# The opening of a two-layer diffusion block: the last 512 tokens loaded later, the modulation in four column groups, new orders on the engines

## The chip, the core and the metric

The kernel runs on one core of a Trainium2 chip. The metric is the device time of one execution in microseconds (us); three runs before the change gave 2850.42, 2852.49 and 2852.70, so the median is 2852.49. Engines: PE (TensorE, matrix products), DVE (VectorE), ACT (ScalarE), POOL (GpSimd) and SP (SyncE, which issues the transfers). PEld in the profile is PE's weight load.

## The reference

Two layers run on 1280 tokens of 1024 features, 256 of them context tokens and 1024 latent tokens. What bears on the change is the head of a layer:

```python
mod = silu_c @ w_ada[l] + b_ada[l]
sh1, sc1, g1, sh2, sc2, g2 = jnp.split(mod[:, None, :], N_MOD, axis=-1)
h = rmsnorm(x, norm1_g[l]) * (1.0 + sc1) + sh1
y, yc = token_mixers(h @ w_in[l], hc @ w_in[l], ...)
x = x + g1 * (y @ w_out[l])
```

The context goes through the same weights, with a modulation vector of its own. The mixers are a two-directional mLSTM, whose keys, values and gates are columns of `w_in`, and a neighbourhood attention. After them come the output projection, a squared-ReLU MLP of 4096 features with the other half of the modulation, and at the end a last RMSNorm. Everything is computed in fp32.

## The kernel before

Activations lie with features on the partitions: x is held in tiles of 128 features. Tokens come in three groups: group 0 is the 256 context tokens, group 1 the next 512, group 2 the last 512. In units of 128 tokens there are ten token tiles, in five pairs i = 0 to 4; pair 0 is group 0, pairs 1 and 2 are group 1, pairs 3 and 4 group 2. An fp32 product of activations and weights is made of three products of rounded parts (L94, L95, L96): the high part of each factor (`ah`, `whi`: a rounding copy on ACT) and the rest (`al`, `wlo`: a subtraction on DVE), without low times low.

The opening (function `opening`) is the stretch up to the first products of the mixers. It runs in layer 0 alone, in a part where each compute engine executes in the order in which the code is written. Its work:

- x is loaded in six transfers (L1566): x_146 and x_147 are group 0 (512 KB each), x_148 and x_149 group 1 and x_150 and x_151 group 2 (1024 KB each); the first of each pair holds features 0 to 511, which the code calls A, the other features 512 to 1023, B.
- Weights of keys, values and gates (`w_kvg`) come in three chunks (L1624, L1688), of 432, 432 and 288 KB, and are split into `whi` (L88) and `wlo` (L89).
- The modulation (`ada`) has two generators. `first` makes the shift and scale of A, `second` those of B. Each has eight k-steps: a load of 512 KB (`wada`, L169) into a ring of six buffers, and products with silu (L158) of 32 columns of PE. Here one k-step is two column groups with 512 columns each. I call the k-steps f0 to f7 and s0 to s7. Then come a copy of the sum (`arow`, L180), four transposes (L183), the addition of the bias (L187) and the gain (L220).
- `squares` (L1639 on ACT, L1640 on DVE, L1641 on PE with a matrix of ones) and `rstd` (L279, L280 on ACT) give the factor of each token; `scale` (L1646, DVE) multiplies it on, eight tiles per group.
- `norm` applies the modulation, in turns on ACT (L1658) and DVE (L1656), and makes the high part (L1094, ACT) and the low part (L1095, DVE).
- `project_g` multiplies pairs of token tiles by 288 columns, 12 products per tile and half of the features. Pairs 0, 1 and 2 are projected in the opening, in PSUM banks tagged "q"; pairs 3 and 4 in the mixers, in banks tagged "mm".

The mixers begin with two small transfers of silu to DRAM (`sscr`, L1572: 1024 elements each, 4 KB, written one 4-byte element at a time from 128 partitions), further modulation work (`fill`, four blocks of 256 columns per load, products in "q" banks), the tables of cosines and sines, and the keys: DVE applies the rotation (L450 to L454), PE transposes (L507), ACT copies.

On SP the built order is not quite the order of the code: a load that waits for a buffer is placed later, and issues written after it can stand ahead of it. Once placed, SP issues one after the other.

Of the kernel before, what the change touches and what calls it, by code (L numbers as in the profile page):

```python
# [11 lines left out]
F32 = mybir.dt.float32  # L12
# [14 lines left out]
KT = D // 128  # L27
# [14 lines left out]
def xf(x, gi, f, o=0, n=None):  # L42

    n = n or GROUPS[gi][1]
    return x[gi][f][:, o:o + n] if len(x[gi]) == KT else x[gi][f // 4][:, f % 4, o:o + n]


class Kern:
# [93 lines left out]
    def ada(self, l, blocks, tag, pool=None, bufs=1):  # L142

        nc, d, ws = self.nc, self.d, []
        pool, nb = pool or self.cp, len(blocks)
        if 0 in blocks:
            self.mod, self.A = self.cp.tile([128, 48, 2], F32, name="mod", bufs=2), {}
        mod = self.mod
        acc = self.bank(tag)
        n = 1024 // nb  # L150
        todo = [(k, o) for o in range(0, 512, n) for k in range(KT)]

        two = 2 if bufs == 1 else 1

        def through(k, o, w):
            for z in range(two):
                for j in range(nb):
                    nc.tensor.matmul(acc[32 * j:32 * j + 32, o:o + n], self.silu[:, k + z, :], w[:, z, j, :], start=k + z == 0, stop=k + z == KT - 1,  # L158
                                     skip_group_check=True, tile_position=(0, 32 * j))

        for i in range(0, len(todo) + bufs * two, two):
            if i >= bufs * two:
                through(*todo[i - bufs * two], ws.pop(0))
            if i < len(todo):
                k, o = todo[i]
                w = pool.tile([128, two, nb, n], F32, name="wada", bufs=bufs)
                for z in range(two):
                    src = d["w_ada"][l, (k + z) * 128:(k + z + 1) * 128, :].rearrange("p (b c) -> p b c", c=512)
                    nc.sync.dma_start(w[:, z], src[:, blocks[0]:blocks[-1] + 1:blocks[1] - blocks[0], o:o + n])  # L169
                    if z < two - 1:  # L170
                        yield
                ws.append(w)
            yield
        m = 32 * len(blocks)
        if bufs == 1:
            row = pool.tile([128, two, nb, n], F32, name="wada")
            rv = row[:].rearrange("p z b c -> p (z b c)")
        else:
            rv = pool.tile([128, 512], F32, name="arow")
        nc.vector.tensor_copy(rv[:m, :512], acc[:m, :])  # L180
        tp = self.bank(tag)
        for t in range(4):
            nc.tensor.transpose(tp[:, t * m:(t + 1) * m], rv[:m, t * 128:(t + 1) * 128], self.ident[:m, :m])  # L183
        for j, b in enumerate(blocks):
            src = tp[:, :4 * m].rearrange("p (t c) -> p t c", t=4)[:, :, 32 * j:32 * j + 2]
            fs = slice(4 * b, 4 * b + 4)
            nc.vector.tensor_add(mod[:, fs, :], src, self.bada[l][:, fs].unsqueeze(2).to_broadcast([128, 4, 2]))  # L187
            for v in range(2):
                self.gain(l, b, v)
        yield  # L190
# [270 lines left out]
    def mlstm_kv(self, l, hi, lo, W, accs):  # L461

        self.kv_begin(0)
        for i in range(NT // 2):
            ga = accs[i] if i in accs else self.project_g(W, i, hi, lo)
            for u in range(2):
                self.nc.scalar.copy(self.gr[:, 2 * i + u, :, 0:8], ga[u][:, 256:288].rearrange("p (q h) -> p q h", q=4))
            self.kv_take(0, i, ga)
            if i > 1:
                self.kv_turn(0, i - 2)  # L470
            yield
        self.kv_turn(0, NT // 2 - 2)
        self.kv_turn(0, NT // 2 - 1)
        yield
        for i in range(NT // 2):
            self.kv_weigh(0, i)
            self.kv_state(0, i)
            yield
        self.kv_back(0)
        yield  # L480
# [1131 lines left out]
    def opening(self, xp, ap0, xsrc, hi, lo):  # L1612


        nc, d = self.nc, self.d
        self.wide, self.ntmp = 0, 8
        x = self.alloc_x(xp, (0, 1, 2))
        self.setup()
        self.load_x(x, xsrc, (0, 1, 2))
        chunks, raws = ((0, 864), (864, 864), (1728, 576)), []  # L1620
        for o, n in chunks:
            raws.append(self.wp.tile([128, 1024], F32, name="wraw", bufs=WRAW) if o < 1728 else ap0.tile([128, n], F32, name="wraw2"))
        for z in range(2):
            nc.sync.dma_start(raws[z][:, :864], d["w_kvg"][0][:, z * 864:z * 864 + 864])  # L1624
        first, second = (self.ada(0, blocks, "mm", ap0, 6) for blocks in ((0, 2), (1, 3)))

        def steps(g, n):
            for _ in range(n):
                next(g)

        steps(first, 6)

        def squares(gi, q):
            p, n = self.bank("mm"), GROUPS[gi][1]
            q.extend((p, n))
            for f in range(0, KT, 2):
                sq = [self.sp.tile([128, 512], F32, name="tmp", bufs=self.ntmp) for _ in range(2)]
                for z, t in enumerate(sq):
                    nc.scalar.activation(t[:, :n], xf(x, gi, f + z), AF.Square)  # L1639
                nc.vector.tensor_add(sq[0][:, :n], sq[0][:, :n], sq[1][:, :n])  # L1640
                nc.tensor.matmul(p[:, :n], self.ones[:], sq[0][:, :n], start=f == 0, stop=f == KT - 2)  # L1641
                yield

        def scale(gi, r, fs=range(KT)):
            for f in fs:
                nc.vector.tensor_mul(xf(x, gi, f), xf(x, gi, f), r[:, :GROUPS[gi][1]])  # L1646

        def norm(todo):

            sh = self.mod[:, 0:8, :]  # L1650

            def modulation(gi, f):
                xs, v = xf(x, gi, f), 1 if gi == 0 else 0
                a, b = self.A[0][:, f, v:v + 1], sh[:, f, v:v + 1]
                if f % 2:
                    nc.vector.tensor_scalar(xs, xs, a, b, ALU.mult, ALU.add)  # L1656
                else:
                    nc.scalar.activation(xs, xs, AF.Identity, bias=b, scale=a)  # L1658

            modulation(*todo[0])  # L1660
            for n, (gi, f) in enumerate(todo):
                if n + 1 < len(todo):
                    modulation(*todo[n + 1])
                self.normed = self.parts(xf(x, gi, f), hi[f][gi][:], lo[f][gi][:])

        q, A, B, accs = [[], [], []], range(4), range(4, 8), {}
        run_all(squares(0, q[0]))
        run_all(squares(1, q[1]))
        r0 = self.rstd(*q[0])
        rest = squares(2, q[2])  # L1670
        steps(rest, 2)
        r1 = self.rstd(*q[1])
        scale(0, r0)
        steps(first, 1)
        steps(rest, 1)
        steps(first, 1)
        steps(rest, 1)
        for z in range(2):
            self.less_last(raws[z], chunks[z][1], 288)
        r2 = self.rstd(*q[2])  # L1680
        scale(1, r1)
        W = [self.split_raw(raws[z], chunks[z][1]) for z in range(2)]
        scale(2, r2, range(6))
        for z in range(6):
            steps(first, 1)
            steps(second, 1)
            if z == 3:
                nc.sync.dma_start(raws[2][:], d["w_kvg"][0][:, 1728:])  # L1688
        steps(first, 1)
        norm([(gi, f) for gi in range(2) for f in A])  # L1690
        scale(2, r2, range(6, 8))
        self.less_last(raws[2], chunks[2][1], 288)
        W.append(self.split_raw(raws[2], chunks[2][1]))
        steps(second, 3)
        accs[0] = self.project_g(W, 0, hi, lo, "q", ks=A, us=(0,))
        steps(second, 1)
        self.project_g(W, 0, hi, lo, "q", accs[0], A, (1,))

        steps(second, 4)
        accs[1] = self.project_g(W, 1, hi, lo, "q", ks=A, us=(0,))  # L1700
        steps(second, 1)
        self.project_g(W, 1, hi, lo, "q", accs[1], A, (1,))
        accs[2] = self.project_g(W, 2, hi, lo, "q", ks=A)
        norm([(gi, f) for gi in range(2) for f in B])
        norm([(2, f) for f in (*A, *B)])
        for i in range(3):
            self.project_g(W, i, hi, lo, "q", accs[i], B)
        return W, accs, self.value_weights(0, range(1))

    def run(self):  # L1710
# [147 lines left out]
def run_all(g):  # L1858
    for _ in g:
        pass  # L1860
# [148 lines left out]
```

## Time and profile before

| what | us |
|---|---|
| median of three runs | 2852.49 |
| the profiled execution's own time | 2852.3 |
| its span from first to last instruction | 2850.2 |
| PE busy in it | 2808.8 (99%) |
| DVE busy | 2199.9 (77%) |
| ACT busy | 1276.3 (45%) |
| first modulated x (L1658) | 38.25 |
| first projection (L94) | 40.30 |
| first modulated x of B (L1656) | 51.56 |

The mean granted clock of PE is 0.997. The rows of the timeline give start, duration, engine, line, operation, tiles, shapes, and in brackets the idle time of the engine just before with what ended it. A row with "x4" joins four like instructions, whose duration is then the sum or the stretch they cover.

### The profile page before, as it was taken

The numbers are of one execution on the slowest core, as the hardware profiler recorded it, in microseconds if no ns is written. First come the engines' busy times: TensorE is split into PE (matmuls) and PEld (weight loads), VectorE is DVE, ScalarE is ACT, GpSimd is POOL, SyncE is SP. The second block draws the span as 40 slices with busy tenths as digits, with TensorE's granted clock in tenths as the row PEclk, the third lists the DMA queues.
The fourth block names the chain that finished last, engine by engine and source line by source line (L and its number), as shares of the span: only waits on it lengthen the run. The fifth ranks groups of instructions, "written<-read, shape, count | busy, mean of one in ns | idle before, by whom it ended". The sixth has DMA issues, their size and how long they took to land. (4 is left out here: it accounts for less than half of the span.)

```text
span 2850.2 us, 45474 instructions
## 1 busy us (share of the span) xinstructions
PE 2808.8 (99%) x16500; PEld 2371.3 (83%) x16500; DVE 2199.9 (77%) x4909; ACT 1276.3 (45%) x2472; POOL 111.5 (4%) x191
## 2 busy tenths in 40 slices
PE   8999999999999999999999999999999999999998
PEld 4877778888888888888889988878888788888888
DVE  6779988776698777689878778878776887768774
ACT  5333335564553333444545333336564533344453
POOL 0110000011000000000000101000020000000000
PEclk9999999999999999999999999999999999999999
DMA  8433433336347555798977222223345454479672
GB/s 259 144 117 120 143 100 101 92 120 212 133 150 245 197 188 201 244 351 292 325 259 272 72 79 88 71 71 119 118 151 197 131 183 158 142 263 319 205 253 96
DMA packets 279264, 497.40 MB, mean 175 GB/s; under 512 B 23648, under 2 KB 119904, under 8 KB 279040
## 3 DMA queue, kind: packets, MB, share of 16 engines
q1 hardware_dynamic: 279040, 494.50, 51.9%
q8 instruction: 130, 2.13, 0.3%
q14 instruction: 94, 0.77, 0.1%
HBM read 398.82 MB, written 95.59 MB: 173 GB/s over the span
## 5 line engine op out<-in xcount | busy, mean ns | idle before, releaser
L94 PE MATMUL q<-ah,whi 128*128 128x512 f32 (+1 forms) x1472 | 549.4, 373 | 0.3 <-ACT whi L1094 0.3
L96 PE MATMUL q<-ah,wlo 128*128 128x512 f32 (+1 forms) x1472 | 547.0, 372 | 0.7 <-DVE wlo L1095 0.5
L95 PE MATMUL q<-al,whi 128*128 128x512 f32 (+1 forms) x1472 | 547.6, 372 | 0.0
L94 PE MATMUL mm<-ah,whi 128*128 128x512 f32 (+1 forms) x1120 | 387.1, 346 | 0.4 <-DVE nq L841 0.2
L95 PE MATMUL mm<-al,whi 128*128 128x512 f32 (+1 forms) x1120 | 384.8, 344 | 0.0
L96 PE MATMUL mm<-ah,wlo 128*128 128x512 f32 (+1 forms) x1120 | 384.6, 343 | 0.0
L94 PE MATMUL mm<-whi,ah 128*128 128x512 f32 (+2 forms) x864 | 317.9, 368 | 1.5 <-ACT va L792 1.5
L96 PEld LDWEIGHTS q<-ah,wlo 128*128 128x128 f32 x1472 | 277.2, 188 | 50.0 <-DVE wlo L1095 1.3
L94 PEld LDWEIGHTS q<-ah,whi 128*128 128x128 f32 x1472 | 277.4, 188 | 49.6 <-issue 1.7
L95 PEld LDWEIGHTS q<-al,whi 128*128 128x128 f32 x1472 | 277.5, 189 | 48.3 <-issue 1.4
L95 PE MATMUL mm<-wlo,ah 128*128 128x512 f32 (+2 forms) x864 | 307.4, 356 | 1.8 <-DVE wlo L89 1.7
L96 PE MATMUL mm<-whi,al 128*128 128x512 f32 (+2 forms) x864 | 307.2, 356 | 0.0
L94 PEld LDWEIGHTS mm<-ah,whi 128*128 128x128 f32 x1120 | 212.0, 189 | 28.2 <-issue 2.0
L96 PEld LDWEIGHTS mm<-ah,wlo 128*128 128x128 f32 x1120 | 212.0, 189 | 25.1 <-issue 0.2
L95 PEld LDWEIGHTS mm<-al,whi 128*128 128x128 f32 x1120 | 212.0, 189 | 24.7 <-issue 0.2
L1094 ACT CAST ah<-raw 128x512 fp32r<-128x512 f32 (+1 forms) x264 | 143.4, 566 | 124.1 <-PE q L96 51.5
L94 PEld LDWEIGHTS mm<-whi,ah 128*128 128x128 f32 x864 | 163.0, 189 | 27.5 <-ACT va L792 2.1
L96 PEld LDWEIGHTS mm<-whi,al 128*128 128x128 f32 x864 | 163.0, 189 | 23.8
L95 PEld LDWEIGHTS mm<-wlo,ah 128*128 128x128 f32 x864 | 163.3, 189 | 22.7 <-DVE wlo L89 3.1
L1095 DVE TENSOR_TENSOR al<-raw,ah 128x512 fp32r<-128x512 f32 (+1 forms) x264 | 157.4, 620 | 30.1 <-ACT ah L1094 29.9
L94 PE MATMUL q<-th,whi 128*128 128x512 f32 x384 | 150.3, 392 | 2.1 <-DVE s L1259 2.0
L95 PE MATMUL q<-x,whi 128*128 128x512 f32 x384 | 150.6, 392 | 1.1 <-DVE x L1095 1.1
(306 smaller groups left out, 5177.3 us busy)
## 6 DMA issues: line engine op xcount, KB each, us to landing
raw<-w SPq DMA_DIRECT2D x168, 512.0 KB
raw<-hid SPq DMA_DIRECT2D x104, 512.0 KB
wada<-w_adaT SPq DMA_DIRECT2D x96, 512.0 KB
wraw<-w SPq DMA_DIRECT2D x80, 512.0 KB
hid<-hb SPq DMA_DIRECT2D x128, 256.0 KB
hid<-ht SPq DMA_DIRECT2D x96, 256.0 KB
w<-gscr SPq DMA_DIRECT2D x36, 512.0 KB
wada<-w_ada SPq DMA_DIRECT2D x32, 512.0 KB
```

The lines of the kernel that those rows point to most:

```text
L94: mm(out, lh, rh, start=start, stop=False, skip_group_check=True)
L95: mm(out, lh, rl, start=False, stop=False, skip_group_check=True)
L96: mm(out, ll, rh, start=False, stop=stop, skip_group_check=True)
L1094: ins = self.nc.scalar.copy(hi, src)
L1095: self.nc.vector.tensor_sub(lo, src, fview(hi))
```

## The change

1. x_150 and x_151 (group 2) and the third chunk of `w_kvg` are loaded after eight loads of the modulation's first half.
2. A generator with two blocks now uses four column groups with 256 columns each, where it used two with 512. The copy is 128x256, and two transposes of 128x128 take the place of four.
3. The orders of all engines are written anew. The squares of group 2 stand on ACT behind the norms of groups 0 and 1 for A; on PE its four sums of squares are interleaved with projections for A and with s0 to s2. The third chunk's low part and three of the scales of group 2 follow, then the end of `second`. For B, norm and projection go group by group; the other five scales of group 2 stand after the norm of group 1, ahead of the norm of group 2.
4. Pair 3 is projected in the opening, with the two token tiles in turns. Pair 4 uses "q" banks, in both layers.

```diff
@@ ada: through
+            if nb == 2:
+                for g in range(4):
+                    nc.tensor.matmul(acc[32 * g:32 * g + 32, 0:256], self.silu[:, k, :], w[:, 0, g // 2, g % 2 * 256:g % 2 * 256 + 256], start=k == 0, stop=k == KT - 1,
+                                     skip_group_check=True, tile_position=(0, 32 * g))
+                return
@@ ada: end
-            rv = pool.tile([128, 512], F32, name="arow")
+            rv = pool.tile([128, 256], F32, name="arow")
+            nc.vector.tensor_copy(rv[:], acc[:, 0:256])
+            tp = self.bank(tag)
+            for t in range(2):
+                nc.tensor.transpose(tp[:, t * 128:(t + 1) * 128], rv[:, t * 128:(t + 1) * 128], self.ident)
...
@@ mlstm_kv
-            ga = accs[i] if i in accs else self.project_g(W, i, hi, lo)
+            ga = accs[i] if i in accs else self.project_g(W, i, hi, lo, "q" if i else "mm")
@@ opening
-        self.load_x(x, xsrc, (0, 1, 2))
+        self.load_x(x, xsrc, (0, 1))
...
+        def project(i, ks, u):
+            accs[i] = self.project_g(W, i, hi, lo, "q", accs.get(i), ks, (u,))
...
+        steps(first, 1)
+        self.load_x(x, xsrc, (2,))
+        nc.sync.dma_start(raws[2][:], d["w_kvg"][0][:, 1728:])
...
+        norm([(0, f) for f in A])
+        for u in range(2):
+            project(0, A, u)
+        rest = squares(2, q[2])
+        norm([(1, f) for f in A])
+        for i in (1, 2):
+            for u in range(2):
+                steps(rest, 1)
+                project(i, A, u)
+                steps(second, 1)
+        r2 = self.rstd(*q[2])
         W.append(self.split_raw(raws[2], chunks[2][1]))
-        steps(second, 3)
...
+        steps(second, 4)
+        scale(2, r2, range(3))
         steps(second, 1)
...
+        norm([(0, f) for f in B])
+        for u in range(2):
+            project(0, B, u)
+        norm([(1, f) for f in B])
+        for i in (1, 2):
+            for u in range(2):
+                project(i, B, u)
+        scale(2, r2, range(3, KT))
+        norm([(2, f) for f in range(KT)])
+        accs[3] = [self.bank("mm") for _ in range(2)]
+        for k in range(KT):
+            for u in range(2):
+                project(3, (k,), u)
         return W, accs, self.value_weights(0, range(1))
```

Line numbers in the order of the changed kernel are its own: L1584 is the load of x, L174 that of w_ada, L1590 the small transfer, L1657 the square, L1676 and L1674 the modulation on ACT and DVE, L1112 and L1113 the high and low parts, L1664 the scale, L185 the copy.

SP's issues from the loads of group 2 on, before:

```order
L1566 DMA x_150<-xT 128x4x512
L1566 DMA x_151<-xT 128x4x512
L1624 DMA wraw<-w_kvg 128x864 x2
L169 DMA wada<-w_ada 128x2x512 x12
L1688 DMA wraw_176<-w_kvg 128x576
L169 DMA wada<-w_ada 128x2x512 x4
L74 DMA wraw<-w_nv 128x1024
L1572 DMA sscr<-silu 128x8x1 x2
L169 DMA wada<-w_ada 128x4x256 x2
```

and with the change, from the first weights on:

```order
L1642 DMA wraw<-w_kvg 128x864 x2
L174 DMA wada<-w_ada 128x2x512 x8
L1584 DMA x_150<-xT 128x4x512
L1584 DMA x_151<-xT 128x4x512
L1698 DMA wraw_174<-w_kvg 128x576
L174 DMA wada<-w_ada 128x2x512 x6
L1590 DMA sscr<-silu 128x8x1 x2
L174 DMA wada<-w_ada 128x4x256
L174 DMA wada<-w_ada 128x2x512 x2
L74 DMA wraw<-w_nv 128x1024 x2
```

The 2 MB of group 2 have moved behind f7. The last two loads of the modulation, s6 and s7, which stood ahead of the two small transfers, now stand behind them and behind one load of the fill.

ACT, from the norm of group 1 for A to the norm of group 0 for B, with the change:

```order
L1112 CAST ah_91<-x_148 128x512
L1112 CAST ah_94<-x_148 128x512
L1112 CAST ah_97<-x_148 128x512
L1657 ACTIVATE tmp<-x_150 128x512 x4
L1657 ACTIVATE tmp<-x_151 128x512 x4
L297 ACTIVATE ssq<-mm,eps 128x512
L298 ACTIVATE ssq<-ssq 128x512
L88 CAST whi<-wraw_174 128x576
L1676 ACTIVATE x_147<-x_147,mod,A_333 128x256
```

The eight squares of group 2 and its factor stand here; before, they stood ahead of all norms, directly behind the squares of group 1.

DVE, from the last low parts of group 1 for B to the first of group 2, with the change:

```order
L1113 TENSOR_TENSOR al_130<-x_149,ah_106 128x512
L1113 TENSOR_TENSOR al_133<-x_149,ah_109 128x512
L1664 TENSOR_TENSOR x_150<-x_150,ssq 128x512
L1664 TENSOR_TENSOR x_151<-x_151,ssq 128x512 x4
L1674 TENSOR_SCALAR x_150<-x_150,A_333,mod 128x512
L1113 TENSOR_TENSOR al_113<-x_150,ah_89 128x512
```

Of the five scales in the middle, three stood ahead of the first half's copy in before, and two ahead of the third chunk's low part, so all of them ahead of the norms of B.

More of the change, by code (lines that the diff above doesn't have):

```diff
@@ L178, in ada @@
         else:
-            rv = pool.tile([128, 512], F32, name="arow")
+            rv = pool.tile([128, 256], F32, name="arow")
[3 more added lines that the diff above has]
+                nc.tensor.transpose(tp[:, t * 128:(t + 1) * 128], rv[:, t * 128:(t + 1) * 128], self.ident)
+            for j, b in enumerate(blocks):
+                fs = slice(4 * b, 4 * b + 4)
+                src = tp[:, 0:256].rearrange("p (t j h c) -> p j h t c", t=2, j=2, h=2)[:, j, :, :, 0:2]
+                nc.vector.tensor_add(mod[:, fs, :].rearrange("p (h t) v -> p h t v", h=2), src,
+                                     self.bada[l][:, fs].rearrange("p (h t) -> p h t", h=2).unsqueeze(3).to_broadcast([128, 2, 2, 2]))
+                for v in range(2):
+                    self.gain(l, b, v)
+            yield
+            return
         nc.vector.tensor_copy(rv[:m, :512], acc[:m, :])
@@ L1666, in opening @@
         q, A, B, accs = [[], [], []], range(4), range(4, 8), {}
+        def project(i, ks, u):
+            accs[i] = self.project_g(W, i, hi, lo, "q", accs.get(i), ks, (u,))
         run_all(squares(0, q[0]))
-        run_all(squares(1, q[1]))
+        more = squares(1, q[1])
+        steps(more, 2)
         r0 = self.rstd(*q[0])
-        rest = squares(2, q[2])
-        steps(rest, 2)
+        steps(more, 1)
+        steps(first, 1)
+        steps(more, 1)
+        steps(first, 1)
+        self.load_x(x, xsrc, (2,))
+        nc.sync.dma_start(raws[2][:], d["w_kvg"][0][:, 1728:])
         r1 = self.rstd(*q[1])
         scale(0, r0)
[L1674 to L1677, printed above, removed]
         for z in range(2):
             self.less_last(raws[z], chunks[z][1], 288)
-        r2 = self.rstd(*q[2])
-        scale(1, r1)
+        scale(1, r1, A)
         W = [self.split_raw(raws[z], chunks[z][1]) for z in range(2)]
-        scale(2, r2, range(6))
+        scale(1, r1, B)
         for z in range(6):
@@ L1686, in opening @@
             steps(second, 1)
-            if z == 3:
-                nc.sync.dma_start(raws[2][:], d["w_kvg"][0][:, 1728:])
+        self.less_last(raws[2], chunks[2][1], 288)
         steps(first, 1)
-        norm([(gi, f) for gi in range(2) for f in A])
-        scale(2, r2, range(6, 8))
-        self.less_last(raws[2], chunks[2][1], 288)
+        norm([(0, f) for f in A])
[9 more added lines that the diff above has]
+        r2 = self.rstd(*q[2])
         W.append(self.split_raw(raws[2], chunks[2][1]))
-        steps(second, 3)
-        accs[0] = self.project_g(W, 0, hi, lo, "q", ks=A, us=(0,))
+        steps(second, 4)
+        scale(2, r2, range(3))
         steps(second, 1)
[L1697 to L1707, printed above, removed]
+        norm([(0, f) for f in B])
[11 more added lines that the diff above has]
+                project(3, (k,), u)
         return W, accs, self.value_weights(0, range(1))
```

## The prediction

> **What bounds the kernel now.** I read the page's busy shares first, then the table of 10-us windows of the opening, then what PE waited for.
>
> ```profile
> PE 2808.8 (99%) x16500; PEld 2371.3 (83%) x16500; DVE 2199.9 (77%) x4909; ACT 1276.3 (45%) x2472; POOL 111.5 (4%) x191
> ```
> ```profile
> core 0: us, PE busy (x) PEld busy (x) DVE busy (x) ACT busy (x) POOL busy (x), PEclk, DMA share, GB/s
> 20.00:30.00 10.00, 8.34 (x18) 1.78 (x20) 8.07 (x15) 2.01 (x5) 0.77 (x1) 0.66 1.02 373
> 30.00:40.00 10.00, 6.91 (x36) 1.84 (x32) 7.54 (x15) 3.36 (x8) 0.09 (x1) 1.00 0.91 307
> 40.00:50.00 10.00, 10.00 (x55) 5.60 (x54) 7.82 (x14) 4.97 (x10) 2.80 (x4) 1.00 0.86 205
> 50.00:60.00 10.00, 10.00 (x77) 9.77 (x76) 7.15 (x20) 7.68 (x15) 1.37 (x6) 1.00 0.74 178
> 60.00:70.00 10.00, 9.93 (x76) 9.69 (x75) 9.13 (x21) 8.08 (x21) 0.65 (x2) 1.00 0.19 63
> 70.00:80.00 10.00, 10.00 (x77) 9.79 (x77) 5.90 (x21) 4.53 (x14) 0.65 (x2) 1.00 0.12 45
> ```
> ```profile
> PE mm L1641 <- DVE tmp L1640: 8.1, 3, 6.6
> PE mm L183 <- DVE arow L180: 3.1, 1, 3.1
> PE mm L158 <- DMA wada<-w_ada: 2.0, 1, 2.0
> PE mm L94 <- ACT va L792: 1.5, 1, 1.5
> ```
>
> PE is the bound nearly everywhere, so the whole kernel moves by as much as the point moves at which PE has finished the opening. All idle time of note lies before 40 us: PE waits for the first squares, for the first modulation load, and for the copy of the modulation (L180). From 40 to 80 us PE is full; nothing saved elsewhere counts unless it moves that stretch. The change touches only this opening, so I follow both programs to one common point: the end of the key, value and gate projection of the last pair of token tiles, i=4. In the profile it stands just ahead of the row at 79.69 below; from there on both programs have the same order.
>
> **The first modulation comes earlier.**
>
> ```profile
> 21.29 1.05 PE L158 MATMUL mm<-wada,silu 128*32 128x512 f32 x4 [1.98 <-DMA wada<-w_ada]
> 36.41 0.67 DVE L180 COPY arow<-mm 64x512 f32<-64x512 f32 x1
> 38.25 0.60 ACT L1658 ACTIVATE x<-x,mod,A 128x256 f32<-128x256 f32 x1 [6.61 <-DVE A L220]
> 40.30 0.40 PE L94 MATMUL q<-whi,ah 128*128 128x288 f32 x1
> ```
> ```profile
> GB/s 0 141 317 381 384 388 389 386 386 388 386 410 403 386 388 386 388 385 380 303 48 333 341 328 343 379 410 376 324 380 106 6 34 25 53 34 97 369 391 226
> ```
> ```profile
> wada<-w_ada SPq DMA_DIRECT2D x18, 512.0 KB
> x<-xT SPq DMA_DIRECT2D x4, 1024.0 KB
> wraw<-w_kvg SPq DMA_DIRECT2D x2, 432.0 KB
> consts<-consts SPq DMA_DIRECT2D x1, 142.0 KB
> ```
>
> The GB/s row covers 0 to 60 us in slices of 1.5 us. It moves 0.69 MB by 4.5 us and then about 0.387 MB per us. As a check on before: ahead of and with the first modulation load go 0.145 MB of constants, 5.24 of x, 0.885 of w_kvg and 0.524 of w_ada, 6.80 MB; (6.80 - 0.69)/0.387 + 4.5 = 20.3 us. Its product starts at 21.29, so about 1.0 us lies between the last byte and its use. After the change the eighth load of the first half (f7) has 0.145 + 3.15 + 0.885 + 8 x 0.524 = 8.37 MB up to its end, which gives 19.8 + 4.5 + 1.0 = 25.3 us. In before, the copy at 36.41 leads to the first modulated x at 38.25 (1.84 us) and to the first projection at 40.30 (2.05 more). The new copy is 256 wide (by 0.41 us, the 128x256 DVE row below, against 0.67, 0.26 less). So: f7 in 25.3, product and semaphores 0.8, copy to modulation 1.6: 27.7 us, and the first projection at 29.8. That is 10.5 us ahead of before.
>
> **What then stands in PE's way: the squares of the last 512 tokens.** They now stand on ACT behind the norms of groups 0 and 1 (features A), and PE's next instruction after the first group's projection is their sum.
>
> ```profile
> 44.52 0.62 ACT L1094 CAST ah<-x 128x512 fp32r<-128x512 f32 x1 [0.69 <-DVE x L1656]
> 9.63 2.19 ACT L1639 ACTIVATE tmp<-x 128x512 f32<-128x512 f32 x4 [1.43 <-DMA x<-xT]
> 11.55 7.76 PE L1641 MATMUL mm<-tmp,ones 128*128 128x512 f32 x12 [1.16 <-DVE tmp L1640]
> ```
> ```profile
> 45.17 3.63 PE L158 MATMUL mm<-wada,silu 128*32 128x512 f32 x16
> 48.73 0.40 PE L94 MATMUL q<-whi,ah 128*128 128x288 f32 x1
> 86.75 1.07 PE L158 MATMUL q<-wada,silu 128*32 128x256 f32 x16
> 87.75 0.39 PE L94 MATMUL mm<-whi,ah 128*128 128x256 f32 x1
> 59.48 0.29 PE L95 MATMUL q<-wlo,ah 128*128 128x288 f32 x1
> 59.61 0.30 PE L96 MATMUL q<-whi,al 128*128 128x288 f32 x1
> ```
>
> ACT needs 45.14 - 38.25 = 6.9 us for these norms, so it is free at 34.6; from the first square to the first product takes 11.55 - 9.63 = 1.9 us, so PE goes on at 36.5, having waited some 3 us. Then come 4 sums of squares, 4 projection halves (12 products of 0.13 us, 1.6 each) and s0 to s5 of the second half of the modulation. A product of 512 columns costs (48.73 - 45.17)/4 = 0.89 us, the price I take for a sum of squares too: before shows those only at a lower clock. A k-step in four column groups of 256 is shown by the later modulation at 86.75: two k-steps in 1.00 us, 0.50 each. So PE has done s5 at 36.5 + 3.6 + 6.3 + 3.0 = 49.4 us. The four groups save 8 x 0.39 = 3.1 us of PE in the second half, the four sums moved into this stretch cost 3.6: about even.
>
> **The two small writes now stand ahead of the last two loads.** On SyncE, s6 and s7 follow the two transfers of silu (L1572, 4 KB each in 4-byte pieces) and one load of the later modulation; in before those stood behind all sixteen loads.
>
> ```profile
> 40.48 2.16 SPq L1572 DMA_DIRECT2D sscr<-silu  x2
> ```
> ```profile
> DMA packets 11955, 17.37 MB, mean 289 GB/s; under 512 B 2736, under 2 KB 5168, under 8 KB 11952
> ```
>
> In the GB/s row the seven slices from 45 to 55.5 us carry 106, 6, 34, 25, 53, 34 and 97, 0.53 MB, which the usual rate moves in 1.4 us. The DMA share there is not low (0.74 from 50 to 60 with 178 GB/s): the engines are busy with 2048 tiny packets. So they hold up what is behind them by 10.5 - 1.4 = 9.1 us. Bounds: 0 (they might be passed) to 10.5. [...] The GB/s row speaks for the long hold-up, and I take the row.
>
> s5 is in after 0.145 + 5.24 + 0.885 + 0.295 + 14 x 0.524 = 13.9 MB: (13.9 - 0.69)/0.387 + 4.5 + 1.0 = 39.6 us. Adding 9.1 gives 48.7; the load between, s6 and s7 take 1.355 each: s7 is in at 52.8. From there to modulated x the first half's chain gives 27.7 - 25.3 = 2.4: the features of B start at **55.2 us**.
>
> ```profile
> 51.56 0.41 DVE L1656 TENSOR_SCALAR x<-x,A,mod 128x256 f32<-128x256 f32 x1
> 32.80 3.69 DVE L1646 TENSOR_TENSOR x<-x,ssq 128x512 f32<-128x512 f32 x6
> 65.68 1.46 DVE L1095 TENSOR_TENSOR al<-x,ah 128x512 fp32r<-128x512 f32 x2
> 70.24 0.28 DVE L454 TENSOR_TENSOR kt<-ropea,ropeb 128x128 f32<-128x128 f32 x1
> 79.69 0.60 PE L318 MATMUL q<-consts,gr 128*128 128x128 f32 x4
> 80.12 0.38 PE L507 MATMUL q<-consts,kt 128*128 128x128 f32 x2
> ```
>
> In before this point is 51.56: **+3.6**. The 10.5 us won at the start are gone, because B waits for its loads, not for PE.
>
> **From B to the common point.** DVE and ACT alternate over all that is left to norm; in before that takes from 51.56 to 67.14 (the end of the last low part, 65.68 + 1.46), 15.6 us. The same list now holds five of the eight scales of the last group, between the norms of groups 1 and 2, in DVE's own order: 5 x 3.69/6 = **+3.1**. In before all eight scales lay in DVE's slack under 50 us. So the last low part ends at 67.14 + 6.7 = 73.8.
>
> Now PE no longer has a store of work there: it runs dry behind DVE and stands at the transposes of the keys. In before those keys are ready at 70.52, 3.4 us after the last low part, and PE passes the common point at 79.69, 12.55 after it. Now it is 3.4 + six of the eight 128x128 products that follow (0.11 each by the step from 79.69 to 80.12, 0.7) + i=4 itself with 48 x 0.13 = 6.3: 10.4 after it, **-2.1**. DVE can give those 2 us: it is busy for 5.90 of the 10 us from 70 to 80. From there PE is full and the delay is passed on whole.
>
> Sum: 3.6 + 3.1 - 2.1 = **+4.6 us**. The other edits I put at nothing: the projection of i=3 moved into the opening is the same products; its bank change and that of i=4 meet no PE wait in before (bounds -1.5 and +1.5, by the one wait of the list after 37 us, L94 for va); the later modulation starts one step later and has the fill's whole stretch to spare. The profiled execution took 2852.3 us by its own time, the median is 2852.49, so 2852.3 + 4.6 = 2856.9 stands for both; I say **2857**.
>
> **Rivals.** *The early start carries through* (faster). If PE never waits again after 29.8, the point comes 10.5 us earlier, plus 3.6 for the sums and less 3.1 for the four groups: -10, 2842 us. For it: PE at 10.00 in every window from 40 on, so 10 us of PE work ahead of time would all count. Against: that needs B modulated by about 41 us, when s5 has only just landed; and the DVE list alone is 15.6 us long. Half of it, with B near 45, would still be faster.
>
> *No hold-up.* If s6 and s7 pass the small writes, or those are short, PE is the later one: s5 done at 49.4, s6 and s7 1.0, copy and modulation 1.9: B at 52.3, +0.7, and the sum is 0.7 + 3.1 - 2.1 = +1.7: 2854. For it: in before one w_nv load was mixed into those 10 us, so part of the time may be its own.
>
> *Longer, and cold.* The hold-up may be the full 10.5, and PE, which waits in pieces from 49.4 to 55, may restart at a lower clock, as the window from 20 to 30 us shows with 0.66. PE has 9.5 us of B products for groups 0 to 2 and 6.3 for i=3 in the 18.6 us to 73.8; some at half speed takes 2 us more past the slack: 1.4 + 2 more, +8, 2860. [...]
>
> *The column groups do not overlap.* Then a k-step costs 4 x 0.50 = 2.0: eight steps in the second half cost 12 us instead of saving; even with the 3 us of waiting they fill, B comes at about 63 and the sum is +12: 2865. Against it stands the row at 86.75, where four groups do run in 0.50.
>
> **Chances and range.** Forecast 0.47, no hold-up 0.20, longer and cold 0.20, early start 0.09, no overlap 0.04. A measurement of this kernel can tell about 0.2%, 5.7 us, from no change. The early start is the only faster case: 0.09. The slower ones are the fourth, most of the third and a fifth of the forecast, whose own range is 2854 to 2859: 0.04 + 0.17 + 0.11 = 0.32. The rest, 0.59, is within. The range from 2851.5 to 2861 leaves out the early start, the fourth and a little of the third.
>
> **What will show it.** Right: the first modulation (before L1658) near 28 us, the first projection near 30; PE waiting 3 us for the sum of squares near 33 to 36; a stretch of almost no GB/s from 39 to 48; B's modulation at 55; PE waiting for keys near 74. Wrong: s6 and s7 landing before 47, B at 52 or earlier, or PE full through from 37. The sizes to compare are B's start, the end of the last low part (73.8) and the end of i=4 (84.3). If the time comes out 2845 or lower, the step that fails is that B waits for its loads.

## The result, and the profile after

The changed kernel takes 2861.14 us (median of eight executions, 2859.85 to 2865.35); the kernel before, beside it, 2853.27. The ratio is 1.0031, with a 95% interval from 1.0020 to 1.0042: slower by some 9 us, where the forecast was +4.6 us and 2857, with a range up to 2861. The direction was right, the size was half of what came, and the time lies just outside the range. One of the eight executions of before took 3971 us and is left out of the ratio. The ratio is formed within one comparison; from one comparison to the next the median of before moves by up to 4 us (2853.3 here, 2856.8 to 2857.2 in the experiments), so below I compare kernels by ratios and by marks in the traces.

The page and the 10-us windows of the opening, after the change (columns as in the prediction):

```profile
PE 2807.8 (98%) x16560; PEld 2375.8 (83%) x16560; DVE 2201.7 (77%) x4909; ACT 1276.6 (45%) x2472; POOL 111.9 (4%) x191
```
```profile
20.00:30.00 10.00, 5.27 (x45) 1.79 (x38) 8.05 (x18) 2.98 (x7) 0.00 (x0) 0.64 1.05 386
30.00:40.00 10.00, 6.90 (x28) 5.66 (x27) 7.65 (x14) 8.49 (x16) 1.14 (x2) 0.67 1.01 333
40.00:50.00 10.00, 10.00 (x64) 6.81 (x63) 0.46 (x1) 0.00 (x0) 0.00 (x0) 0.84 0.54 69
50.00:60.00 10.00, 7.19 (x65) 4.46 (x64) 5.30 (x14) 4.43 (x10) 3.42 (x3) 1.00 0.75 275
70.00:80.00 10.00, 7.95 (x60) 7.51 (x59) 9.66 (x27) 7.42 (x23) 0.65 (x2) 1.00 0.32 102
```

PE's busy time is the same as before (2808.8); its idle time has grown from 41 to 50 us. From 40 to 50 us PE is full, but DVE and ACT do next to nothing (0.46 and 0.00 us): both wait for PE. The granted clock is 0.67 and 0.84 in two of these windows where before had 1.00, and 0.83 from 60 to 70 us.

The timeline of after, at the places the prediction named:

```profile
28.07 0.60 ACT L1676 ACTIVATE x<-x,mod,A 128x256 f32<-128x256 f32 x1 [6.99 <-DVE A L238]
29.16 0.61 PE L94 MATMUL q<-whi,ah 128*128 128x288 f32 x1 [1.67 <-ACT ah L1112]
35.47 4.26 ACT L1657 ACTIVATE tmp<-x 128x512 f32<-128x512 f32 x8
37.48 2.05 PE L1659 MATMUL mm<-tmp,ones 128*128 128x512 f32 x2 [3.10 <-DVE tmp L1658]
52.41 2.37 PE L158 MATMUL mm<-wada,silu 128*32 128x256 f32 x40
56.91 0.41 DVE L1674 TENSOR_SCALAR x<-x,A,mod 128x256 f32<-128x256 f32 x1
65.05 3.09 DVE L1664 TENSOR_TENSOR x<-x,ssq 128x512 f32<-128x512 f32 x5
74.03 1.47 DVE L1113 TENSOR_TENSOR al<-x,ah 128x512 fp32r<-128x512 f32 x2
86.25 0.38 PE L525 MATMUL q<-consts,kt 128*128 128x128 f32 x2
```

and what the DMA moved, in slices of 1.5 us from 0 to 60:

```profile
GB/s 0 144 318 387 382 384 392 404 401 394 385 388 388 388 385 388 388 384 388 384 395 385 386 384 386 257 29 0 3 57 27 87 182 365 411 401 389 339 34 0
```

| point | before | predicted | after |
|---|---|---|---|
| first modulated x | 38.25 | 27.7 | 28.07 |
| first projection | 40.30 | 29.8 | 29.16 |
| first sum of squares of group 2 | | 36.5 | 37.48 |
| s3 starts on PE | | 47.9 (36.5 + 3.6 + 6.3 + 1.5) | 52.41 |
| B's first modulated x | 51.56 | 55.2 | 56.91 |
| end of the last low part | 67.14 | 73.8 | 75.50 |
| end of i=4 | 79.69 | 84.3 | 86.25 |

Up to the end of i=4 the change costs 6.6 us. Right behind it stands one more pair of transposes than in before, so the next product comes 6.8 us later (87.05 against 80.26). Further on the wait list of PE has a new line:

```profile
PE q L163 <- DMA wada<-w_ada: 2.1, 2, 1.2
```

These are loads of the later modulation. A mark on DVE at 240 us, the first of a group of weighted sums, stands 8.0 us later than before:

```profile
237.87 1.28 DVE L209 CUSTOM_DVE_ANT_0 wada<-wada,consts 128x1024 f32<-128x1024 f32 x1
```
```profile
245.83 1.28 DVE L227 CUSTOM_DVE_ANT_0 wada<-wada,consts 128x1024 f32<-128x1024 f32 x1
```

The first row is before, the second after. This distance doesn't last: before waits 1.7 us for low parts of weights between 250 and 360 us, after 0.3, and a later mark, the tile `qT` on ACT, comes at 356.45 and 362.91, 6.5 us apart. The two profiled executions end 7.6 us apart (2852.3 and 2859.85).

### The profile page after: what moved, and what is told of

It is laid out like the page before. It is cut to its first block, busy times and chain, and to the rows that moved or that the text cites. A ratio compares the mean times of both kernels' runs of the same rounds, so it can differ in the third digit from the quotient of the medians.

```text
span 2857.9 us, 45593 instructions
## 1 busy us (share of the span) xinstructions
PE 2807.8 (98%) x16560; PEld 2375.8 (83%) x16560; DVE 2201.7 (77%) x4909; ACT 1276.6 (45%) x2472; POOL 111.9 (4%) x191
## 5 line engine op out<-in xcount | busy, mean ns | idle before, releaser
L94 PE MATMUL mm<-whi,ah 128*128 128x512 f32 (+2 forms) x832 | 308.0, 370 | 1.6 <-ACT va L810 1.6
L95 PE MATMUL mm<-wlo,ah 128*128 128x512 f32 (+2 forms) x832 | 297.9, 358 | 0.4 <-DVE wlo L89 0.3
L96 PE MATMUL mm<-whi,al 128*128 128x512 f32 (+2 forms) x832 | 297.9, 358 | 0.0
L1112 ACT CAST ah<-raw 128x512 fp32r<-128x512 f32 (+1 forms) x264 | 143.5, 566 | 126.0 <-PE q L96 51.8
L1113 DVE TENSOR_TENSOR al<-raw,ah 128x512 fp32r<-128x512 f32 (+1 forms) x264 | 157.8, 622 | 29.9 <-ACT ah L1112 29.2
L94 PEld LDWEIGHTS mm<-whi,ah 128*128 128x128 f32 x832 | 157.1, 189 | 27.1 <-ACT va L810 2.4
L96 PEld LDWEIGHTS mm<-whi,al 128*128 128x128 f32 x832 | 156.9, 189 | 23.8
L95 PEld LDWEIGHTS mm<-wlo,ah 128*128 128x128 f32 x832 | 157.3, 189 | 21.3 <-DVE wlo L89 1.8
```

The lines of the kernel that those rows point to most:

```text
L94: mm(out, lh, rh, start=start, stop=False, skip_group_check=True)
L95: mm(out, lh, rl, start=False, stop=False, skip_group_check=True)
L96: mm(out, ll, rh, start=False, stop=stop, skip_group_check=True)
L1112: ins = self.nc.scalar.copy(hi, src)
L1113: self.nc.vector.tensor_sub(lo, src, fview(hi))
```

## The experiments

After the first comparison two theories stood against each other. The prediction's: B waits for its loads, which the small writes of silu hold up. Theory 2: B waits for PE. PE stands still until ACT has squared group 2 (3.10 us), then runs at half the clock for some 6 us (0.50 from 36.46 to 43.29), and s3 to s7 stand behind all four sums and all four projections. The quiet in the GB/s row from 39 to 48 us is there as predicted, but in after no wait of PE on a `wada` load follows it: the five last k-steps run through from 52.41 without a break.

### Small writes late, PE kept busy, and both

The first edit, in the mixers:

```diff
-            for v in range(2):
-                self.nc.sync.dma_start(self.sscr[v, :].rearrange("(k p) -> p k", p=128), self.silu[:, :, v])
+            with self.tc.issue_after(next(i for i in reversed(self.nc.cur_bb.bb.instructions) if i.engine == mybir.EngineType.SP)):
+                for v in range(2):
+                    self.nc.sync.dma_start(self.sscr[v, :].rearrange("(k p) -> p k", p=128), self.silu[:, :, v])
```

> The changed kernel with the two small writes of silu issued behind all loads of the opening. Theory of the prediction (B waits for its loads, which the small writes hold up): s7 is in near 45, B starts near 52.3 instead of 56.9, and the time falls by 4 to 5 us. Theory 2 (B waits for PE, which comes late through the sums of squares and through a half clock from 37 to 44 us): s3 still starts near 52.4, B near 56.9, the end of i=4 stays at 86.3; at most 1 us is won, at the fill's loads further on.

Measured: ratio 1.0022 (1.0013 to 1.0032). B at 57.02, end of i=4 at 86.45: nothing moved. Two rows of its timeline show this. The DMA row under them (slices of 1.5 us) shows that the 9 us of hold-up have gone; the rate falls only from 40.5 to 45 us, while SP waits for a buffer to issue s6:

```profile
52.52 2.37 PE L158 MATMUL mm<-wada,silu 128*32 128x256 f32 x40
57.02 0.41 DVE L1675 TENSOR_SCALAR x<-x,A,mod 128x256 f32<-128x256 f32 x1
```
```profile
GB/s 0 131 298 384 387 391 386 397 408 396 382 391 386 388 385 391 385 384 391 386 391 385 392 380 386 380 258 22 0 31 266 376 277 329 366 109 71 120 6 0
```

So the step "B waits for its loads" is wrong for the change as it stands.

The second edit puts products that nothing reads ahead of the first sum:

```diff
         norm([(1, f) for f in A])
+        idle = self.bank("mm")
+        for _ in range(7):
+            nc.tensor.matmul(idle[:, :256], self.ones[:], self.consts[:, :256], start=True, stop=True)
```

> The changed kernel with seven idle products of 256 columns on PE behind the first group's projection, into a bank that nothing reads, so that PE does not rest before the first sum of squares. Theory 2: the granted clock from 37.5 to 44 us is full, s3 starts near 49 instead of 52.4, then the last load (in at about 53.2) sets B: near 55.4, 1.5 us won. Theory of the prediction: PE's pace there does not matter, nothing changes. Third way: the clock falls all the same, since it was low from 22 to 33 us already; then the seven products only cost time.

> Both edits together: small writes late and PE kept busy. Theory 2: now neither the loads nor the clock hold B, s3 starts near 49, B near 53.3, 3.5 us won against the changed kernel. If only the loads mattered it equals the first of these runs, if only the clock did it equals the second.

Measured: kept busy alone 1.0043 (1.0028 to 1.0058), both edits 1.0027 (1.0016 to 1.0037). The windows of the small writes late alone, and of both edits:

```profile
37.50:44.00 6.50, 6.36 (x24) 4.07 (x24) 2.08 (x3) 2.38 (x5) 0.00 (x0) 0.55 0.42 152
```
```profile
37.50:44.00 6.50, 6.50 (x44) 4.70 (x42) 2.08 (x3) 2.27 (x5) 0.00 (x0) 1.00 0.38 109
```

PE does 24 products at clock 0.55 and 44 at 1.00 in the same 6.5 us. From the first sum to s3 it takes 52.52 - 37.64 = 14.9 us against 50.41 - 38.25 = 12.2:

```profile
37.64 2.05 PE L1660 MATMUL mm<-tmp,ones 128*128 128x512 f32 x2 [3.13 <-DVE tmp L1659]
```
```profile
38.25 1.02 PE L1660 MATMUL mm<-tmp,ones 128*128 128x512 f32 x2
50.41 2.37 PE L158 MATMUL mm<-wada,silu 128*32 128x256 f32 x40
```

The low clock costs 2.7 us here. With both edits B comes at 54.92 and the end of i=4 at 84.27: 2.0 us better than after, not the 3.5 expected, because the idle products themselves delay the first sum by 0.6 and the rest of the list is a little longer than I had it. The whole time shows no such gain against the small writes late alone, and in the traces the 2.2 us between these two at the end of i=4 are gone by 293 us (a weighted sum at 293.20 against 292.98); between 64 and 420 us PE waits longer for low parts of weights with both edits (2.8 us against 1.3). Why is open.

Kept busy alone is where the hold-up does bite. SP there put one small write, issued at 41.91, ahead of s7, issued at 44.67; the change issues both writes from 30.48 on, ahead of s6 too:

```profile
50.37 1.93 PE L158 MATMUL mm<-wada,silu 128*32 128x256 f32 x32
56.02 1.08 PE L158 MATMUL mm<-wada,silu 128*32 128x256 f32 x8 [3.71 <-DMA wada<-w_ada]
```

These are PE's rows at its last k-steps. With PE 2 us ahead it now waits 3.7 us for the last load, and B is at 58.98. From 45 to 54 us the DMA moves only 4 to 56 GB/s there. So the prediction's mechanism exists and the quiet stretch is as long as it said; in the change PE was later than the load. The 3.7 us belong to this order of SP; what the wait would be with the change's own order and an earlier PE is not shown.

### One part undone, one part alone: the column groups

> The changed kernel with the modulation in two column groups again (part 2 of the change undone), the rest as it is. Theory 2 (B waits for PE): eight k-steps of s cost 0.39 more each, so B starts 2 to 3 us later than 56.9, near 59.5, and the end of i=4 near 88.5. Theory of the prediction (B waits for its last load, in at 53.2): B moves by at most 1.

The edit takes the `if nb == 2` branch and the new end of `ada` out of the changed kernel. One execution, of 2872.55 us: B at 59.46, end of i=4 at 88.65, the numbers of Theory 2 (59.5 and 88.5); the prediction's theory had at most 1 us.

```profile
51.34 3.63 PE L158 MATMUL mm<-wada,silu 128*32 128x512 f32 x16
56.52 1.05 PE L158 MATMUL mm<-wada,silu 128*32 128x512 f32 x4 [1.54 <-DMA wada<-w_ada]
```

The second row shows that 1.5 us of it is a wait for s7 after all, so this run alone doesn't part the two theories, and that Theory 2 hit both numbers is luck: the low clock that its 56.9 holds is missing here. In its windows the clock from 37.5 to 44 us is 1.00, although PE rested 3.3 us ahead of the first sum, longer than the 3.1 in after (its wait list, then its window):

```profile
PE mm L1641 <- DVE tmp L1640: 3.3, 1, 3.3
```
```profile
37.50:44.00 6.50, 6.13 (x32) 4.15 (x32) 2.31 (x4) 2.62 (x6) 0.00 (x0) 1.00 0.62 76
```

> The kernel before with the four column groups alone (part 2 of the change), everything else as before. From the rows: 8 k-steps of s at 0.50 instead of 0.89 lie in the full stretch of PE, so B starts 3 us earlier (near 48.5) and the end of i=4 comes near 76.6: 3 us faster than before. Rival: the groups do not overlap here, or B then waits for s7 (in at 45.1, B near 47.5 at the earliest) and DVE, so less than 1 us is won.

> The kernel before with the four column groups alone, again, for a narrower interval. By its first trace: the end of i=4 at 77.5 instead of 79.7, and some 1.5 us more from waits that vanish by 350 us: a ratio near 0.9985. The first comparison gave 0.9977 with an interval from 0.9966 to 0.9987.

This is the kernel before with the branch and the new end of `ada` and nothing else. Ratios 0.9977 (0.9966 to 0.9987) and 0.9982 (0.9974 to 0.9991): faster, by 5 to 7 us. B comes at 49.23 and 48.42 (expected 48.5), the end of i=4 at 77.49 and 76.83: 2.2 and 2.9 us ahead.

```profile
44.71 1.93 PE L158 MATMUL mm<-wada,silu 128*32 128x256 f32 x32
77.49 0.60 PE L336 MATMUL q<-consts,gr 128*128 128x128 f32 x4
```

Four k-steps in 1.93 us: 0.48 each, as the later modulation had shown. The traces gain 1.6 to 2.8 us more by 350 us; there before waits 1.7 us for low parts of weights, where the lists of these two runs have none and 0.4. The rival "the column groups do not overlap" is out.

### The scales of group 2

> The changed kernel with the five scales of group 2 that stand between the norms of groups 1 and 2 moved from DVE to POOL, behind the factor. Theory 2: DVE's list from B to the last low part is the path there, so B stays near 56.9, the last low part ends 3.1 us earlier (near 72.4 instead of 75.5) and the end of i=4 comes near 83.2 instead of 86.3. POOL needs some 1.6 us for each (its 128x252 subtraction takes 0.8), so it is done near 62, ahead of the norm of group 2. Rival: that norm is bound by ACT or by PE, then nothing moves; or POOL slows DVE down, then less than 3.

```diff
-        scale(2, r2, range(3, KT))
+        for f in range(3, KT):
+            nc.gpsimd.tensor_mul(xf(x, 2, f), xf(x, 2, f), r2[:, :512])
```

One execution, of 2868.06 us. The rival came true: POOL slows DVE.

```profile
52.65 8.03 POOL L1734 TENSOR_TENSOR x<-x,ssq 128x512 f32<-128x512 f32 x5 [20.31 <-ACT ssq L298]
54.47 5.08 DVE L1664 TENSOR_TENSOR x<-x,ssq 128x512 f32<-128x512 f32 x3
61.28 1.75 DVE L1674 TENSOR_SCALAR x<-x,A,mod 128x256 f32<-128x256 f32 x1
```

A scale takes 1.6 us on POOL (8.03/5), and while POOL runs, one on DVE takes 1.69 us (5.08/3) instead of the 0.62 of after (3.09/5). What holds DVE up is not shown. B starts at 61.28, 4.4 us later, and the end of i=4 is at 88.77.

The size of the scale term needs no experiment of its own. From B's first modulated x to the last low part before takes 15.58 us, after 18.59, the small writes late 18.58, two column groups 18.59. The difference is 3.01, where the prediction had 3.1. With no scale on DVE in that stretch it is 16.70, although the first modulation there, beside a POOL that still fills tiles (two of 1.16 us from 60.62 us on), takes 1.75 us (the third row above) instead of 0.41.

### Another order

> The changed kernel with another order: the squares of group 2 directly behind the norm of group 0, their four sums on PE directly behind the first group's projection, the factor in the middle of the norm of group 1, six of the scales ahead of the second modulation and two behind the norm of group 0 for B, the k-steps of s ahead of the projections of group 1, the small writes behind all loads. Theory 2: PE does not rest before the sums, r2 is there near 39, s7 is in near 46, B starts near 48 and the last low part ends near 64: the end of i=4 near 75.5, 4 us ahead of the kernel before, so about 2848 where that has 2852. If the early start cannot be kept in any order (loads or DVE in the way), it ends at 79 or later.

```diff
-        rest = squares(2, q[2])
-        norm([(1, f) for f in A])
-        for i in (1, 2):
-            for u in range(2):
-                steps(rest, 1)
-                project(i, A, u)
-                steps(second, 1)
-        r2 = self.rstd(*q[2])
+        rest = squares(2, q[2])
+        steps(rest, 4)
+        norm([(1, f) for f in A[:2]])
+        r2 = self.rstd(*q[2])
+        norm([(1, f) for f in A[2:]])
         W.append(self.split_raw(raws[2], chunks[2][1]))
-        steps(second, 4)
-        scale(2, r2, range(3))
-        steps(second, 1)
+        steps(second, 6)
+        for u in range(2):
+            project(1, A, u)
+        scale(2, r2, range(6))
+        steps(second, 3)
+        for u in range(2):
+            project(2, A, u)
         norm([(0, f) for f in B])
         for u in range(2):
             project(0, B, u)
+        scale(2, r2, range(6, KT))
         norm([(1, f) for f in B])
...
-        scale(2, r2, range(3, KT))
```

The ratio is 0.9989 (0.9979 to 0.9998), B at 48.50, the end of i=4 at 75.93. Same loads, same products, same column groups as the change (the small writes late, which alone moved nothing), and that point is 10.3 us earlier. The sums follow the first group's projection without a rest, and k-steps follow them:

```profile
35.15 3.59 PE L1660 MATMUL mm<-tmp,ones 128*128 128x512 f32 x8
38.67 2.80 PE L158 MATMUL mm<-wada,silu 128*32 128x256 f32 x48
```

So the early loads can be kept in gain; the order had lost them.

> As f4, with all eight scales of group 2 on POOL. If DVE's list is the path, the eight scales (0.61 each, 4.9 us in all, of which some filled gaps) leave it: B near 46.5, the end of i=4 near 73.8, 6 us ahead of the kernel before. Rival: POOL, at 1.6 us each, ends behind the norms of group 1 (41 + 13 = 54) and slows DVE, so it is no better than f4.

With all scales on POOL the ratio is 1.001 (1.000 to 1.002), the end of i=4 at 78.16, 2.2 us later than without: again DVE is slower beside POOL (while POOL scales, from 39.91 us on, two low parts at 41 us take 3.45 us instead of 1.29).

> As f4, with the factor of group 2 behind the whole norm of group 1 instead of in its middle (in f4 ACT waited 1.6 us for the sums there and DVE 3.0 us behind it). From f4's rows: DVE's scales start 2 us earlier, B starts near 47.5 instead of 48.5 to 49, the end of i=4 comes near 74.1 instead of 75.9, 5.6 us ahead of before, ratio near 0.998. If the path in f4 was PE and not DVE's list, it stays at 75.9.

```diff
-        norm([(1, f) for f in A[:2]])
-        r2 = self.rstd(*q[2])
-        norm([(1, f) for f in A[2:]])
+        norm([(1, f) for f in A])
+        r2 = self.rstd(*q[2])
```

The small writes are left here to SP's own placing, which puts them behind s7. B at 47.80, the end of i=4 at 74.87 (expected 74.1), ratio 0.9985 (0.9976 to 0.9994). On the same chip the change itself:

> The changed kernel as it is, on the same chip as the two below, for the comparison. Theory 2: the end of i=4 at 86.3 and a ratio to before near 1.003, as in the first comparison.

1.0026 (1.0017 to 1.0034), with the end of i=4 at 86.87. The first comparison repeats in the whole time, though not step by step: from the first sum to s3 this execution takes 13.8 us (37.84 to 51.65, clock 0.74 from 37.5 to 44 us), B comes at 56.16, and the projection of i=4 then runs in part at a low clock (0.80 from 80 to 87 us).

At 240 us the lead over before in this kernel has shrunk from 4.8 to 3.7. The last run is about that:

> As g6, with one more step of the later modulation taken where pair 3 is taken over from the opening (in the change that projection stands in the opening, where the step does nothing, so every later step comes one place later). If this shift is what costs the 1 us between 100 and 250 us (PE waiting 2.1 us for the later modulation's loads, which before does not do), these waits go and the lead of 4.8 us over before at the end of i=4 is still there at 240 us, where g6 has 3.7. Otherwise the waits stay and it equals g6.

```diff
             ga = accs[i] if i in accs else self.project_g(W, i, hi, lo, "q" if i else "mm")
+            if i == 3 and i in accs:
+                self.tick()
```

The ratio is 0.9975 (0.9965 to 0.9985), the best of all, though its interval meets those of the kernel before with four groups and of the run without this line. From the wait lists from 80 to 420 us, first without the line, then with it:

```profile
PE q L163 <- DMA wada<-w_ada: 1.7, 2, 1.0
PE mm L94 <- ACT va L810: 1.6, 1, 1.6
```
```profile
PE mm L94 <- ACT va L812: 1.4, 1, 1.4
PE q L201 <- DVE wada L198: 1.3, 1, 1.3
```

The waits for the loads are gone; a wait for the copy, which before has too (1.1 us, its L183), is back. At 240 us the mark is at 234.17, 3.7 us ahead of before, where the end of i=4 had a lead of 4.2. By the mark on ACT at 356.45 in before the lead is 5.3 with the line (351.19) and 4.4 without it (352.03), where it began at 4.2 and 4.8. So the shift of the later modulation was a cost of its own, 1.5 us up to this point.

## Why the prediction came out as it did

**The first modulation comes earlier: right.** 28.07 and 29.16 against 27.7 and 29.8. The bytes ahead of f7 over the steady rate were enough. The 0.8 us for product and semaphores was an estimate that no row of before gives; in after f7's product starts at 25.06 and the copy at 26.26, 1.2 us later.

**The rest ahead of the sums: right, 1 us short.** PE waited 3.10 us ("some 3"). ACT was free at 35.47, not 34.6, and the first sum came at 37.48.

**"PE has done s5 at 49.4": this step failed.** s3 to s7 ran from 52.41 to 54.8, where the step has s3 at 47.9. Of the 4.5 us 1.0 is the later first sum, 2.7 the low clock from 37.5 to 44 us (by the pair of runs with and without it), and 0.8 the sums and k-steps, which take longer here than the 0.89 and 0.50 read elsewhere (at full clock 3.2 us from one sum to the next, where the prediction has 3.0). Before does show sums at full clock, other than the prediction says: seven of their products of 512 columns, two to a sum, start from 15.71 to 18.72 us, at clock 1.00, and take 0.59 to 0.70 us, against 1.06 at clock 0.50 (23.72). I had priced everything at full clock and kept the low clock for a rival that set in at 49.4, after the wrong rest: PE rested ahead of the sums, and that is where the clock was low.

**"B waits for its loads": wrong as a bound, right in part as a mechanism.** That B comes late was right, for another reason than the one given. The quiet stretch lies from 39 to 48 us, as predicted, and a kernel in which PE came earlier waited 3.7 us for the last load. In the change PE was later than the load, so B came 1.7 us after the 55.2 predicted, and taking the small writes away gave nothing. Two chains of nearly the same length stood there (55.2 by loads, 52.3 by PE in my numbers); 4.5 us on the shorter one turned them round.

The step also left out that the ring has six buffers: s6 and s7 can be issued only when PE is done with s0 and s1. PE ends s1 at 46.64 in after and at 46.74 with the small writes late, and SP issues s7 right behind it in both:

```profile
46.70 0.37 SPq L174 DMA_DIRECT2D wada<-w_ada  x1
```
```profile
46.80 0.37 SPq L174 DMA_DIRECT2D wada<-w_ada  x1
```

So a late PE delays these loads too: with the small writes late this wait alone leaves the DMA quiet from 40.5 to 45 us. And what fills the quiet stretch behind the small writes is not the tiny packets, as the prediction has it. Before from 46.5 to 54 us, then after from 42 to 48:

```profile
DMA packets 380, 0.23 MB, mean 30 GB/s; under 512 B 165, under 2 KB 379, under 8 KB 379
```
```profile
DMA packets 276, 0.26 MB, mean 43 GB/s; under 512 B 23, under 2 KB 276, under 8 KB 276
```

Only 165 and 23 packets of under 512 B are left there, of 2048; a few hundred larger ones, of the loads behind them, keep the 16 engines busy for 55.1% and 51.4% of these stretches. Where nothing is queued behind the writes, they are through soon: with the small writes late they are issued from 56.04 us on, and the GB/s row of that run has 6 from 57 to 58.5 us and 0 from 58.5 to 60. Why the packets behind them take so long stays open.

**Five scales in DVE's list: +3.1, measured 3.0.** The list from B to the last low part: predicted 18.6, measured 18.59.

**From the last low part to the end of i=4:** predicted 10.4, measured 10.75; the 2.1 us given back were 1.8.

**"The other edits I put at nothing": 1.4 us at 240 us, nothing lasting in the trace.** The later modulation starting one step later had "the fill's whole stretch to spare"; PE then waited 2.1 us for its loads, where before has one wait of 1.1 us for a copy, and the mark at 240 us is 8.0 late where the end of i=4 was 6.6. The run with the step put back shows this wait tied to the shift. By 357 us the distance is back at 6.5, as before makes waits of its own. What is left between the traces (7.6 us at their end) and the ratio's 8.8 is inside its interval of 5.7 to 12 us.

Of the rivals, "longer and cold" had the sign, and the size (+8) by luck. PE did run at a low clock again where it had it, behind the waits at B's start (0.66 from 60 to 65 us), but that cost nothing up to the last low part: the list takes 18.57 us in the run kept busy alone too (58.98 to 77.55), where the clock is 0.56 and 0.50 from 55 to 65 us. The clock that cost time was the one ahead of s3. "The early start carries through" describes what the other orders reached in part: 4.8 us at the end of i=4, not 10. In the best of them B's list on DVE still takes 16.5 us (47.80 to 64.32), and no run here shortened it; that it binds there is likely but not shown. Undone in after: from 10.2 us ahead at the first modulation to 5.35 behind at B are 15.5 us. They went into PE's rest (3.1), the low clock (2.7), the sums now in that stretch (4 x 0.9) and the projections, which the prediction has in its sum of PE but not among what undoes the early start: 72 products stand ahead of the copy of B's modulation, where before has 24, and 48 x 0.13 are 6.3 us. The four column groups give 3.1 back. The 2.9 us left are the slow sums (0.8) and, for the most part, group 0's own 24 products, which take 5.2 us (29.16 to 34.38, with the clock at 0.50 up to 33.05) instead of 3.1. Behind B come 3.0 of scales.

## What to carry to other kernels

When a stage starts earlier, follow every chain that meets at its end, PE's own included, and price each with the clock it may have: here a rest of 3.1 us was followed by 2.7 us of lost clock. For a load that waits for a buffer, ask which engine frees the buffer. Where two chains end within a few us of each other, forecast the later of the two with both errors added, not the one that looks later. In an order written by hand, put the work that frees other engines (here sums and factor) ahead of the work that only PE needs, and look at each list that was merely shifted by one place.

## What was not expected of the hardware

In these runs the rest of PE alone did not tell the clock that followed. In after, and with the small writes late, 3.1 us of rest were followed by a granted clock near half (0.55 from 37.5 to 44 us), and in the change run again 2.4 us by 0.74. With two column groups 3.3 us were followed by 1.00, and before itself rests 3.1 us ahead of 37.23 and keeps 1.00 (from 30 to 50 us). In the order without a rest ahead of the sums it was 1.00 from 37.5 to 44 us.

The traces show where the clock changes. From 16 to 100 us it is 0.50 from 22.24 to 29.07 us in before, and from 22.81 to 33.05, 36.46 to 43.29 and 60.35 to 63.76 us in after: 3.41 us each, or two or three times that. Else it is 1.00. The stretch in which most of the rest lies, and the next, in after, in the change run again, and in before (second number: PE busy; third from the end: clock):

```profile
33.05:36.46 3.41, 1.33 (x10) 1.09 (x9) 2.62 (x5) 2.72 (x6) 0.00 (x0) 1.00 1.05 386
36.46:39.87 3.41, 2.39 (x5) 1.39 (x6) 2.18 (x4) 3.27 (x7) 0.00 (x0) 0.50 0.97 242
```
```profile
34.97:38.38 3.41, 1.01 (x7) 0.57 (x5) 2.62 (x5) 3.08 (x6) 0.00 (x0) 1.00 1.05 384
38.38:41.80 3.42, 3.42 (x13) 2.90 (x12) 1.74 (x3) 1.71 (x4) 0.00 (x0) 0.50 0.63 47
```
```profile
32.48:35.90 3.42, 1.66 (x8) 0.23 (x4) 3.42 (x7) 0.00 (x0) 0.00 (x0) 1.00 0.98 337
35.90:39.31 3.41, 2.08 (x12) 0.81 (x14) 2.07 (x7) 1.03 (x3) 0.00 (x0) 1.00 1.02 365
```

Where PE was busy for 1.33 and 1.01 us of such a stretch, the next one has half the clock; in before a border at 35.90, counted on in steps of 3.41 us from the change at 29.07, parts the rest, PE is busy for 1.66 and 2.08, and the clock stays, as it does with two groups (1.62 and 1.89, border at 36.35). So in these four executions the clock went with how the rest lay in these stretches, not with its length; more than that they do not show. A limit in busy time does not come out: from 56.94 to 60.35 us in after PE is busy for 2.35 us, in pieces, and the next stretch has 0.50 all the same.

Scales on POOL made DVE's work beside them slower in the two runs that had them: 1.69 us for a scale on DVE instead of 0.62, with 1.6 us for one on POOL, and 1.73 us for a low part instead of 0.65.
